# Batch-norm with ReLU on one core: all stores from GpSimd's queue, and the rows loaded in rising order

## The chip, the cores and the metric

The kernel runs on one core of one Trainium2 chip. The metric is the device time of one execution in microseconds (us), as the median of several runs. A profile is taken of one execution. Its span runs from the first instruction of the program to the last.

## The reference

The input x has 32 x 128 x 32 x 32 float32 values (16.78 MB). For each channel c the output is

```
normalized = (x - running_mean[c]) / sqrt(running_var[c] + eps)
out = maximum(normalized * gamma[c] + beta[c], 0)
```

So each value is multiplied by a scale of its channel, a bias of its channel is added, and negative values become 0. Every byte of x is read once, and as many are written.

## The kernel before

x is seen as 4096 rows (batch by channel) of 1024 values (4 KB). They are cut in two halves, t = 0 and t = 1, of 128 partitions with J = 16 rows each, so that partition p of half t holds 16 rows that follow each other in memory (64 KB). Row j of all 128 partitions together is 0.52 MB. All of x has its own place in SBUF (32 times 4 KB a partition), the results overwrite it, and no buffer is used twice.

TILES (L16) lists pieces (t, a, b): rows a to b of half t. The order of the list is the order of the loads and of the work: (0, 0, 2), (0, 2, 4), then all of half 1, then (0, 4, 12) and (0, 12, 16). The loads are issued by SP (L56), one DMA a piece, unless LOAD_CUTS cuts it. They are 1, 1, 8, 4 and 2 MB, and SP issues them all within the first 8 us.

Meanwhile four small DMAs on ScalarE's queue (L63) fetch the channels' parameters, a matmul (L78) spreads them over the partitions, and ScalarE's square root (L86) and four VectorE operations (L88 to L94) make scale_t and bias_t, with one column for each j.

Then ScalarE goes through the pieces in order. For each row it runs one ACTIVATE in place (L102), relu(scale * x + bias), of 128 x 1024 values; a row in HALVES is done as two of 128 x 512. After the last row of a piece, and ahead of each row in STORE_CUTS, it issues a DMA of the finished rows to the output (L110). There are seven stores, of 0.5, 0.5, 1, 4, 4, 4 and 2 MB. The order on ScalarE is the order written (manual_schedule, L96). For the other engines a scheduler sets it.

A DMA's share of one partition is one contiguous run (4 KB times its rows). The 16 DMA engines of the core carry all queues: q1 with SP's loads, q10 with ScalarE's DMAs. At the end SP waits for all DMAs (L144), and then all engines pass a barrier.

Of the kernel before, what the change touches and what calls it, by code (L numbers as in the profile page):

```python
# [1 line left out]

# [4 lines left out]


F32 = mybir.dt.float32
ACTF = mybir.ActivationFunctionType  # L10

J = 16

TILES = ((0, 0, 2), (0, 2, 4), (1, 0, 16), (0, 4, 12), (0, 12, 16))  # L16

LOAD_CUTS = set()
STORE_CUTS = {(0, 1), (1, 8)}

HALVES = {(0, 0)}


@with_exitstack
def kernel(
    ctx: ExitStack,
    tc: tile.TileContext,
    x: bass.AP,
    gamma: bass.AP,
    beta: bass.AP,  # L30
    running_mean: bass.AP,
    running_var: bass.AP,
    eps: bass.AP,
    out: bass.AP,
):
    nc = tc.nc
    B, C, H, W = x.shape
    HW = H * W
    P = nc.NUM_PARTITIONS
    assert C % J == 0 and P % (C // J) == 0 and (B * C) % (P * J) == 0  # L40
    Q = C // J
    T = B * C // (P * J)

    xr = x.rearrange("b c h w -> (b c) (h w)").rearrange("(t p j) w -> t p j w", p=P, j=J)
    outr = out.rearrange("b c h w -> (b c) (h w)").rearrange("(t p j) w -> t p j w", p=P, j=J)

    data = ctx.enter_context(tc.tile_pool(name="data", bufs=1))
    params = ctx.enter_context(tc.tile_pool(name="params", bufs=1))
    psum = ctx.enter_context(tc.tile_pool(name="psum", bufs=1, space=bass.MemoryType.PSUM))

    tiles = []
    for t, a, b in TILES:
        xt = data.tile([P, b - a, HW], F32, name=f"x{t}_{a}")
        cuts = [a] + [j for j in range(a + 1, b) if (t, j) in LOAD_CUTS] + [b]
        for c, d in zip(cuts, cuts[1:]):
            nc.sync.dma_start(out=xt[:, c - a : d - a, :], in_=xr[t, :, c:d, :])  # L56
        tiles.append((t, a, b, xt))

    raw = params.tile([Q, 4, J], F32, name="raw")
    for k, src in enumerate((running_var, gamma, running_mean, beta)):
        nc.scalar.dma_start(out=raw[:, k, :], in_=src.rearrange("(q j) -> q j", j=J))  # L63
    eps_t = params.tile([P, 1], F32, name="eps_t")
    nc.vector.memset(eps_t, float(eps))  # L65
    rep = params.tile([Q, P // Q, Q], F32, name="rep")
    nc.gpsimd.memset(rep, 1.0)  # L67
    nc.gpsimd.affine_select(  # L68
        out=rep,
        in_=rep,  # L70
        compare_op=mybir.AluOpType.is_equal,
        fill=0.0,
        base=0,
        pattern=[[0, P // Q], [-1, Q]],
        channel_multiplier=1,
    )
    cols = psum.tile([P, 4, J], F32, name="cols")
    nc.tensor.matmul(  # L78
        cols.rearrange("p k j -> p (k j)"),
        rep.rearrange("q r s -> q (r s)"),  # L80
        raw.rearrange("q k j -> q (k j)"),
        start=True,
        stop=True,
    )
    std_t = params.tile([P, J], F32, name="std_t")
    nc.scalar.activation(out=std_t, in_=cols[:, 0, :], func=ACTF.Sqrt, bias=eps_t[:, 0:1], scale=1.0)  # L86
    rstd_t = params.tile([P, J], F32, name="rstd_t")
    nc.vector.reciprocal(out=rstd_t, in_=std_t)  # L88
    scale_t = params.tile([P, J], F32, name="scale_t")
    nc.vector.tensor_mul(out=scale_t, in0=cols[:, 1, :], in1=rstd_t)  # L90
    ms_t = params.tile([P, J], F32, name="ms_t")
    nc.vector.tensor_mul(out=ms_t, in0=cols[:, 2, :], in1=scale_t)  # L92
    bias_t = params.tile([P, J], F32, name="bias_t")
    nc.vector.tensor_sub(out=bias_t, in0=cols[:, 3, :], in1=ms_t)  # L94

    with tc.manual_schedule(engines={mybir.EngineType.Activation}):  # L96
        for t, a, b, xt in tiles:
            first = a
            for j in range(a, b):
                step = HW // 2 if (t, j) in HALVES else HW  # L100
                for w in range(0, HW, step):
                    nc.scalar.activation(  # L102
                        out=xt[:, j - a, w : w + step],
                        in_=xt[:, j - a, w : w + step],
                        func=ACTF.Relu,
                        bias=bias_t[:, j : j + 1],
                        scale=scale_t[:, j : j + 1],
                    )
                if j + 1 == b or (t, j + 1) in STORE_CUTS:
                    nc.scalar.dma_start(  # L110
                        out=outr[t, :, first : j + 1, :], in_=xt[:, first - a : j + 1 - a, :]
                    )
                    first = j + 1


# [1 line left out]
_INS = ['x', 'gamma', 'beta', 'running_mean', 'running_var', 'eps']  # L117
_OUTS = [((32, 128, 32, 32), 'float32')]

_NUMBERS = {'eps': 1e-05}  # L120


# [26 lines left out]
```

## Time and profile before

| | |
|---|---|
| median of 7 runs | 83.98 us (83.89 to 84.2) |
| the profiled execution | 83.83 us |
| its span | 82.1 us |
| ScalarE busy | 38.8 us (47%) |
| ScalarE, 33 ACTIVATEs of L102 | 37.3 us |
| VectorE, TensorE, GpSimd busy | under 1 us each |
| read and written | 16.78 MB and 16.78 MB |
| mean rate over the span | 409 GB/s |

How to read it: the profile's engine rows count compute alone. A DMA is seen in three other places: the instruction that issues it (under half a microsecond on its queue), the packets that the 16 DMA engines move later, and the landing, when its semaphore has its full count and a waiting instruction can go on. From issue to landing a 4 MB store here takes 19.6 us, since it waits for its turn.

### The profile page before, as it was taken

The page shows a single profiled execution, that of the slowest core. Times are in us where ns is not written, and L with a number is a line of the kernel's source. Part 1 is how long each engine was busy: PE and PEld are TensorE (multiplying, and loading weights), DVE is VectorE, ACT ScalarE, POOL GpSimd, SP SyncE. Part 2 cuts the span into 40 slices and gives each one's busy share as a digit, 9 for nine tenths or more (in the row PEclk, how much of TensorE's full clock was granted, in tenths as well). Part 3 has the DMA queues.
Part 4 walks back from the last instruction along what each step waited for, and adds up shares of the span by engine and source line. Part 5 has one row for each costly group of instructions (what it writes and reads, how often), then busy time and mean ns, then how long its engine had stood idle before and what let it go on. Part 6 is the DMA issues. An engine that isn't in the chain of part 4 may idle for free.

```text
span 82.1 us, 119 instructions
## 1 busy us (share of the span) xinstructions
PE 0.7 (1%) x2; PEld 0.5 (1%) x2; DVE 0.8 (1%) x5; ACT 38.8 (47%) x35; POOL 0.8 (1%) x6
## 2 busy tenths in 40 slices
PE   0002000000000000000000000000000000000000
PEld 0002000000000000000000000000000000000000
DVE  0000300000000000000000000000000000000000
ACT  0600377600000199997999989997991000000000
POOL 3000000000000000000000000000000000000000
DMA  1999990999929797969989998996996998997992
GB/s 40 367 419 707 511 511 0 511 543 543 447 96 543 319 511 319 575 287 455 407 359 463 519 399 367 511 495 271 511 511 271 495 511 351 415 511 343 423 407 104
DMA packets 1792, 33.56 MB, mean 409 GB/s; under 512 B 256, under 2 KB 256, under 8 KB 512
## 3 DMA queue, kind: packets, MB, share of 16 engines
q1 hardware_dynamic: 720, 16.78, 48.7%
q10 hardware_dynamic: 1072, 16.78, 47.6%
HBM read 16.78 MB, written 16.78 MB: 409 GB/s over the span
## 4 chain that ended last, share of the span: by engine, by line
ACT 37%; DMA 33%; issue 3%; ACTq 1%; SPq 1%
ACT x L102 37%; DMA x<-in_x_dram 33%; ACTq L110 1%; SPq L56 1%
## 5 line engine op out<-in xcount | busy, mean ns | idle before, releaser
L102 ACT ACTIVATE x<-x,bias_t,scale_t 128x1024 f32<-128x1024 f32 (+1 forms) x33 | 37.3, 1205 | 15.9 <-DMA x<-in_x_dram 12.7
L86 ACT ACT_TABLE_LOAD x1 | 1.3, 1283 | 2.6 <-issue 2.6
L86 ACT ACTIVATE std_t<-cols,eps_t 128x16 f32<-128x16 f32 x1 | 0.3, 274 | 4.5 <-PE cols L78 4.5
L78 PE MATMUL cols<-raw,rep 8*128 8x64 f32 x2 | 0.7, 430 | 7.7 <-DMA raw<-in_beta_dram 7.7
L78 PEld LDWEIGHTS cols<-raw,rep 8*128 8x128 f32 x2 | 0.5, 308 | 7.7 <-issue 7.7
L68 POOL TENSOR_SCALAR_AFFINE_SELECT rep<-rep 8x128 f32<-8x128 f32 x1 | 0.4, 394 | 0.1
L88 DVE RECIPROCAL rstd_t<-std_t 128x16 f32<-128x16 f32 x1 | 0.3, 253 | 7.8 <-ACT std_t L86 7.8
L67 POOL MEMSET rep<- 8x128 f32 x1 | 0.2, 196 | 0.3 <-POOLq L130 0.3
L90 DVE TENSOR_TENSOR scale_t<-cols,rstd_t 128x16 f32<-128x16 f32 x1 | 0.2, 175 | 0.1
L92 DVE TENSOR_TENSOR ms_t<-cols,scale_t 128x16 f32<-128x16 f32 x1 | 0.2, 175 | 0.0
L94 DVE TENSOR_TENSOR bias_t<-cols,ms_t 128x16 f32<-128x16 f32 x1 | 0.2, 175 | 0.0
L130 POOL MEMSET const-bfloat16-1.0<- 128x1 bf16 x1 | 0.1, 107 | 0.0
L130 POOL MEMSET const-uint8-127<- 128x1 uint8 x1 | 0.1, 107 | 0.0
L130 POOL MEMSET const-float32-0.0<- 128x1 f32 x1 | 0.1, 104 | 0.3 <-issue 0.3
L130 POOL MEMSET const-float32-1.0<- 128x1 f32 x1 | 0.1, 104 | 0.0
L65 DVE MEMSET eps_t<- 128x1 f32 x1 | 0.1, 59 | 0.9 <-PEq L130 0.9
## 6 DMA issues: line engine op xcount, KB each, us to landing
out_dram<-x ACTq DMA_DIRECT2D x3, 4096.0 KB, 19.6
x<-in_x_dram SPq DMA_DIRECT2D x1, 4096.0 KB
x<-in_x_dram SPq DMA_DIRECT2D x2, 1024.0 KB, 5.6
x<-in_x_dram SPq DMA_DIRECT2D x1, 2048.0 KB
out_dram<-x ACTq DMA_DIRECT2D x1, 2048.0 KB, 19.4
out_dram<-x ACTq DMA_DIRECT2D x2, 512.0 KB, 21.2
out_dram<-x ACTq DMA_DIRECT2D x1, 1024.0 KB, 31.6
raw<-in_running_var_dram ACTq DMA_DIRECT2D x1, 0.5 KB
```

What stands on the lines that cost most here:

```text
L56: nc.sync.dma_start(out=xt[:, c - a : d - a, :], in_=xr[t, :, c:d, :])
L67: nc.gpsimd.memset(rep, 1.0)
L68: nc.gpsimd.affine_select(out=rep, in_=rep, compare_op=mybir.AluOpType.is_equal, fill=0.0, base=0, pattern=[[0, P // Q], [-1, Q]], channel ...
L78: nc.tensor.matmul(cols.rearrange("p k j -> p (k j)"), rep.rearrange("q r s -> q (r s)"), raw.rearrange("q k j -> q (k j)"), start=True, s ...
L86: nc.scalar.activation(out=std_t, in_=cols[:, 0, :], func=ACTF.Sqrt, bias=eps_t[:, 0:1], scale=1.0)
L88: nc.vector.reciprocal(out=rstd_t, in_=std_t)
L90: nc.vector.tensor_mul(out=scale_t, in0=cols[:, 1, :], in1=rstd_t)
L92: nc.vector.tensor_mul(out=ms_t, in0=cols[:, 2, :], in1=scale_t)
L94: nc.vector.tensor_sub(out=bias_t, in0=cols[:, 3, :], in1=ms_t)
L102: nc.scalar.activation(out=xt[:, j - a, w : w + step], in_=xt[:, j - a, w : w + step], func=ACTF.Relu, bias=bias_t[:, j : j + 1], scale=sc ...
L110: nc.scalar.dma_start(out=outr[t, :, first : j + 1, :], in_=xt[:, first - a : j + 1 - a, :])
L130: nc = _bacc.Bacc("TRN2", target_bir_lowering=False, num_devices=1)
```

## The change

All stores are issued by GpSimd (POOL) in place of ScalarE, in an order that is written out, too. The pieces now rise in size: (0, 0, 2), (0, 2, 4), (0, 4, 8), (0, 8, 16), and then all of half 1. Half 1 is loaded by two DMAs of 8 rows (LOAD_CUTS). Loads are 1, 1, 2, 4, 4 and 4 MB. The cut (1, 8) leaves STORE_CUTS, so there are six stores, of 0.5, 0.5, 1, 2, 4 and 8 MB, and the last of them holds all 16 rows of half 1. Row 1 of half 0 is done in two halves, like row 0.

```
-TILES = ((0, 0, 2), (0, 2, 4), (1, 0, 16), (0, 4, 12), (0, 12, 16))
+TILES = ((0, 0, 2), (0, 2, 4), (0, 4, 8), (0, 8, 16), (1, 0, 16))
 
-LOAD_CUTS = set()
-STORE_CUTS = {(0, 1), (1, 8)}
+LOAD_CUTS = {(1, 8)}
+STORE_CUTS = {(0, 1)}
 
-HALVES = {(0, 0)}
+HALVES = {(0, 0), (0, 1)}
...
-    with tc.manual_schedule(engines={mybir.EngineType.Activation}):
+    with tc.manual_schedule(engines={mybir.EngineType.Activation, mybir.EngineType.Pool}):
...
                 if j + 1 == b or (t, j + 1) in STORE_CUTS:
-                    nc.scalar.dma_start(
+                    nc.gpsimd.dma_start(
                         out=outr[t, :, first : j + 1, :], in_=xt[:, first - a : j + 1 - a, :]
                     )
```

## The prediction

> **What bounds the kernel now.** I read the page's slices and queues first, to see whether the DMA engines ever rest.
>
> ```profile
> DMA  1999990999929797969989998996996998997992
> ...
> q1 hardware_dynamic: 720, 16.78, 48.7%
> q10 hardware_dynamic: 1072, 16.78, 47.6%
> HBM read 16.78 MB, written 16.78 MB: 409 GB/s over the span
> ```
>
> q1 carries the loads, which SP issues, and q10 the stores, which ScalarE issues. Together their packets take 96.3% of 82.1 us on all 16 engines: 39.98 us of loads and 39.08 us of stores, 79.06 us in all. (A 0 or 2 in a slice is no hole. A large packet is counted where it starts.) The first load packet starts at about 1.7 us. 1.7 + 79.1 = 80.8, and what is left to 82.1 is the end of the program. So **the DMA engines are full from the first load to the last store**. The kernel is bound by the sum of its transfers. The chain of waits seems to say otherwise:
>
> ```profile
> 1.71 26.71 DMA x<-in_x_dram
> ...
> 57.19 0.13 ACT x L102
> 57.32 1.02 issue
> 58.34 3.49 ACT x L102 x3
> ```
>
> It ends at 61.8 us, with the last store's ScalarE work, because the chain follows engines and not queues. The 20 us behind it are stores that wait for their turn. ScalarE idles 12.7 us before the 8 MB load lands at 28.4 us, which costs nothing as long as the queues are full.
>
> Then I read the queues by stretches, for the price of a packet and for how the two queues share an engine. The columns are packets, MB, and time as a share of 16 engines in the stretch. 10 to 28.4 us, then 28.4 to 38.6, then 38.6 to 46.9, then 56.8 to 82.1:
>
> ```profile
> q1 hardware_dynamic: 128, 6.82, 87.5%
> q10 hardware_dynamic: 96, 0.39, 5.2%
> ```
> ```profile
> q1 hardware_dynamic: 114, 3.67, 83.5%
> q10 hardware_dynamic: 124, 0.44, 10.6%
> ```
> ```profile
> q1 hardware_dynamic: 158, 2.10, 63.1%
> q10 hardware_dynamic: 216, 1.59, 45.3%
> ```
> ```profile
> q10 hardware_dynamic: 416, 9.96, 91.3%
> ```
>
> MB divided by share times stretch gives rates: loads of tile 1 (64 KB of a partition in a packet) 6.82 / 16.1 us = 424 GB/s; loads mostly of rows 4 to 12 (32 KB) 3.67 / 8.52 = 431; loads of rows 12 to 16 (16 KB) 2.10 / 5.24 = 401; stores of 4 KB 0.39 / 0.957 = 407 and 0.44 / 1.08 = 407; large stores alone 9.96 / 23.1 = 431. One engine has a sixteenth, so a 32 KB packet takes 32768 / 26.9 = 1.22 us and a 4 KB one 0.16 us. In the second stretch the queues' times stand 83.5 to 10.6, or 7.9 to 1, and the packets 8 to 1 in size. So **each engine takes one packet of each queue in turn**, and a queue of small packets gets little. That is why the loads are nearly done at 46.9 us while most stores wait.
>
> **The change, part by part.** The bytes are the same: 16.78 MB in, 16.78 MB out.
>
> *Load order and sizes.* Tile 1 now comes last, as two 4 MB loads, and the first half as 1, 1, 2 and 4 MB. The 64 KB load packets go, and 8.39 MB of 32 KB packets stands for them. At 431 instead of 424 GB/s this is 19.79 - 19.46 = 0.33 us less. Mixed with stores, though, the 16 KB loads ran at 401 GB/s, so loads vary by more than this with what runs beside them. I bound the load side by -0.7 us (16 KB loads at full rate as well: 2.10 MB at 431 saves 0.37) and +0.4 us (that loss repeated), and take 0.
>
> *When each row is ready.* Loads alone end at 1.7 + 40.0 = 41.7 us. Store packets are taken from about 11.3 us, when ScalarE finishes row 0. From there some 26 load packets are left (24 of 32 KB, 2 of 16 KB), so at most 26 store packets come between: 16 of 4 KB (0.16 us each), 8 of 8 KB (0.31) and 2 of 16 KB (0.62), 6.3 us in all. The loads end by 48.0 us and have landed by 48.5 (in the trace of before the last load packet ends near 46.0 and its semaphore is full at 46.4). ScalarE, at 9.16 / 8 = 1.145 us a row, has done the other 24 rows: rows 8 to 16 of the first half land near 23 us and are done near 32, the next eight land near 34 and are done near 43. The last eight take until 48.5 + 9.2 = 57.7.
>
> *The last store.* STORE_CUTS loses (1, 8), so all of tile 1 leaves by one 8.39 MB store that waits for the last row, at 57.7 us. Is there work for the engines until then? Loads and the five earlier stores (8.39 MB, half of 39.08) keep them full to 1.7 + 40.0 + 19.5 = 61.2 us. With 0.4 us for the issue (ScalarE's stores take 0.34 to 0.37) and 1 us to the first packet (SP's first load is issued at 0.81 us and moves at 1.7), the store's packets are there at 59.1, so **2 us are to spare and nothing is lost**. The same cover hides the new wait. If it is gone, each us later costs one us. Behind the waiting stores on POOL stand only later stores, since its own work ends at 1.5 us.
>
> *Issue from POOL.* Seven issues of 0.34 to 0.37 us, and five pauses between rows (2.2 us in the list of waits), leave ScalarE. They are worth nothing, since ScalarE isn't on the path; what is late next is the DMA queue, as before. POOL's six issues have no row. I bound one by 0.1 us (POOL's shortest work) and 0.59 us (the longest issue in the trace, a parameter load's). Both stay under the cover above; I take 0.4. SP's six loads still leave early: the fifth and sixth wait for a parameter load and for the first x load, as the last two did before (3.6 and 1.5 us in SP's waits), with over 8 MB queued ahead of them.
>
> *Store packets from POOL's queue.* Before has no transfer from this queue. From below, they are as ScalarE's: 431 GB/s, 0 us (nothing in the trace ran faster). From above, all are as the 4 KB ones: 16.78 / 0.407 = 41.2 us against 39.1, so +2.1 us. The shapes are those of ScalarE's stores (4 KB to 64 KB of a partition), so I take the near row, 0, and keep +2.1 for the range. The Trainium skill, "DMA: Bandwidth & Descriptors", section Latency and other measured facts, says that DMA engines 7 and 15 are usually slower for GpSimd's transfers, with a cause that it calls a guess. In this trace no engine has such transfers, and by this rule the sum would gain an unknown part of a store's time on two engines.
>
> *The end of the program.* SP waits for every DMA semaphore before the last barrier.
>
> ```profile
> L144 SPq EVENT_SEMAPHORE  x7: 17/28/28, 57.1 to 82.1; - x7
> L144 POOLq DRAIN  x3: 34/77/489, 1.0 to 81.9; - x3
> L144 SPq DRAIN  x3: 7/7/7, 81.4 to 81.7; - x3
> ```
>
> Five of the seven are such waits, and the last store is the last of them. In the instruction order of the changed program there are eight, the last store's is the first, and seven follow it: 28 ns each is 0.2 us, and with the gap to the drain that follows the last wait now (about 65 ns from start to start) 0.46 us. I take **+0.35 us**. A longer drain of POOL's queue adds between 0 and 0.4 us (489 for 77 ns); I take 0.
>
> **Sum:** 0 + 0 + 0 + 0.35 = +0.35 us on the profiled 83.83 us (span 82.1, and 1.73 around it, which stay), 84.18. The median of the runs is 0.15 above the profiled one, so 84.33, say **84.3 us, +0.4%**.
>
> **Rivals.**
>
> *Loads get cheaper (faster), 83.6 us.* The load side gives its -0.7 us and the end costs 0.35: -0.35. For it speaks that stores kept their rate and only loads varied (401 to 431). Against it, that loads beside stores are no rarer in the new order.
>
> *Stores run in poorer packets, 86.4 us.* +2.1 + 0.35. For it: nothing shows how POOL's queue cuts a row. Against it: the same contiguous runs gave packets of their full size on two other queues. Half of the loss gives 85.4.
>
> *The stores take more than a packet in a turn (slower), 95.4 us.* This is a stall at one place, ahead of the 8.39 MB store. If the stores get two packets or more for each load packet, all five earlier ones (40 packets an engine, 20 turns) fit among the 26 load packets. The loads then end when all else is done, at 61.2 us. The engines idle for 0.5 (landing) + 9.2 (eight rows) + 1.4 (issue, first byte) = 11.1 us, and the time is 83.98 + 11.1 + 0.35 = 95.4. It decides from loads that end after about 50 us. Against it: the 7.9 to 1 above. For it: that ratio is of ScalarE's queue, and POOL's is another. The Trainium skill, "DMA: Bandwidth & Descriptors", section Queues, rings and completion order, says that an engine empties a whole packet of one ring before it turns, and that a packet has 9 to 17 descriptors typically. By the page a store's share on one engine (8 partitions) would be one turn, and the sum would be this rival's; by the row of before, with one descriptor a turn, it is 84.3.
>
> *Nothing to measure, 84.0 us.* The end's cost and a load gain of 0.3 cancel.
>
> **How the numbers follow.** A difference under 0.2% (0.17 us) can't be told from none here. Chances: forecast 0.38 (84.1 to 84.7; 0.05 of it lies within 0.2%), cheaper loads 0.26, poorer packets 0.16, stall 0.12, nothing 0.08. Slower: 0.33 + 0.16 + 0.12 = 0.61. Same: 0.05 + 0.08 = 0.13. Faster: 0.26. The range from 83.3 (load side at its best) to 86.5 (all packets as 4 KB ones) leaves out the stall and a little below, some 0.17. The likeliest case alone is 84.1 to 84.7.
>
> **What would show it.** Right: DMA busy for 79 us without a hole, loads done before 50 us, the 8.39 MB store issued near 56 to 58 us, seven waits of SP behind the last landing. Wrong: an empty slice before the last store (stall); a store rate under 431 GB/s, or packets smaller than a row group (poorer packets); a load share under 48% of the span (cheaper loads).

## The result and the profile after

The changed kernel takes 84.39 us (median of 14 runs, 84.21 to 84.56) against 83.99 (37 runs of before). The ratio is 1.0044, 95% interval 1.0034 to 1.0054. The forecast was 84.3. The profiled execution took 84.40 us, with a span of 82.7.

The page's slices and queues of the changed kernel:

```profile
ACT  0600499994059998299991299991000000000000
POOL 3000032202000000200000000002000000000000
DMA  1999996979696969797998999899699569999900
...
q1 hardware_dynamic: 864, 16.78, 48.3%
q0 software_dynamic: 864, 16.78, 47.2%
q10 hardware_dynamic: 64, 0.00, 0.0%
```

The stores are on q0 now, and only the parameters are left on q10. Loads take 48.3% of 82.69 us, 39.96 us (before 40.01 in the trace's own sum), and stores 39.0 (before 39.0). Counted packet by packet, at least 16 packets, as many as there are engines, are under way at every moment from 3 us to 78.5 us, shortly before the last packets start, so no gap is seen there. The bound is the same as before.

The last store's cover held, as the rows of POOL and ScalarE show:

```profile
23.71 9.16 ACT L102 ACTIVATE x<-x,bias_t,scale_t 128x1024 f32<-128x1024 f32 x8 [4.28 <-DMA x<-in_x_dram]
33.16 0.53 POOL L110 DMA_DIRECT2D out_dram<-x  x1 [12.90 <-ACT x L102]
34.65 9.16 ACT L102 ACTIVATE x<-x,bias_t,scale_t 128x1024 f32<-128x1024 f32 x8 [1.78 <-DMA x<-in_x_dram]
46.93 9.16 ACT L102 ACTIVATE x<-x,bias_t,scale_t 128x1024 f32<-128x1024 f32 x8 [3.13 <-DMA x<-in_x_dram]
56.38 0.53 POOL L110 DMA_DIRECT2D out_dram<-x  x1 [22.69 <-ACT x L102]
```

Groups of eight rows start at 23.7, 34.7 and 46.9 us, and the last store is issued at 56.4. Its first packet moves at 61.24, when the store ahead of it is through on the first engine.

How the two queues share an engine, in the stretches 28.4 to 38.6 and 56.8 to 82.1 us:

```profile
q1 hardware_dynamic: 141, 4.10, 93.2%
q0 software_dynamic: 133, 0.54, 13.0%
```
```profile
q0 software_dynamic: 209, 9.99, 91.2%
```

93.2 to 13.0 is 7.2 to 1, for 32 KB packets beside 4 KB ones (and a few of 8 KB at the end of the stretch). POOL's queue too gets one packet for one. 9.99 MB in 23.07 us is 433 GB/s, and in the trace all 128 packets of 64 KB took 2418 ns. So POOL's packets are neither poorer nor more in a turn.

The end of the program grew. In the next rows an EVENT_SEMAPHORE of SP is one of its waits, a DRAIN is an instruction at which an engine stops near its end, and RANGE_CLEAR is POOL's clearing of the semaphores. The three figures are the shortest, median and longest in ns, then come the first and last start in us. The instructions of L144:

```profile
L144 SPq EVENT_SEMAPHORE  x10: 17/28/46762, 34.6 to 82.6; - x10
L144 POOLq EVENT_SEMAPHORE  x4: 17/17/17, 82.0 to 82.6; - x4
L144 POOLq DRAIN  x3: 34/102/25311, 56.4 to 82.4; - x3
L144 SPq DRAIN  x3: 7/7/7, 81.9 to 82.2; - x3
L144 POOLq EVENT_SEMAPHORE_RANGE_CLEAR  x1: 139/139/139, 82.3 to 82.3; - x1
```

SP's first wait lasts 46.8 us, up to the last store's landing at 81.38 us. Then come seven more, which start 59 to 68 ns apart, and SP's drain starts at 81.89, 0.51 us after the landing; in before it started at 81.37, 0.08 us after the landing. From the last landing to the end of the span it is 1.31 us in place of 0.83, **0.48 us more**. Another line matters later: POOL's own drain starts at 56.4 us and lasts 25.3 us, until 81.67, 0.29 us after the landing. So it too waits for the store. Two rows of before stand against these:

```profile
L144 ACTq DRAIN  x2: 8/80/153, 62.2 to 81.7; - x2
L144 POOLq EVENT_SEMAPHORE_RANGE_CLEAR  x1: 96/96/96, 81.7 to 81.7; - x1
```

ScalarE's drain in before starts at 62.2 us, with its stores under way until 81, and lasts 0.15 us: it does not wait for them. The clearing of the semaphores took 96 ns there and takes 139 now.

### The profile page after: what moved, and what is told of

It is laid out like the page before. It is cut to its first block, busy times and chain, and to the rows that moved or that the text cites. A ratio compares the mean times of both kernels' runs of the same rounds, so it can differ in the third digit from the quotient of the medians.

```text
span 82.7 us, 125 instructions
## 1 busy us (share of the span) xinstructions
PE 0.7 (1%) x2; PEld 0.5 (1%) x2; DVE 0.8 (1%) x5; ACT 38.7 (47%) x36; POOL 4.2 (5%) x12
## 3 DMA queue, kind: packets, MB, share of 16 engines
q1 hardware_dynamic: 864, 16.78, 48.3%
## 4 chain that ended last, share of the span: by engine, by line
DMA 56%; issue 11%; POOLq 1%
DMA x<-in_x_dram 56%; POOLq L144 1%; POOLq L110 0%
## 5 line engine op out<-in xcount | busy, mean ns | idle before, releaser
L110 POOL DMA_DIRECT2D out_dram<-x x6 | 3.4, 559 | 52.1 <-ACT x L102 52.1
```

The source lines that it names most:

```text
L110: nc.gpsimd.dma_start(out=outr[t, :, first : j + 1, :], in_=xt[:, first - a : j + 1 - a, :])
```

## The experiments

Every run gives the ratio to before with its 95% interval. "The end" is the time from the last landing to the end of the span in the run's own trace (before: 0.83 us).

| run | stores from | us | ratio | the end, us |
|---|---|---|---|---|
| changed kernel | POOL | 84.39 | 1.0044 (1.0034 to 1.0054) | 1.31 |
| e9, the same again | POOL | 84.41 | 1.0050 (1.0037 to 1.0063) | 1.31 |
| e1 changed order | ScalarE | 83.52 | 0.9942 (0.9923 to 0.9961) | 0.83 |
| e8, the same again | ScalarE | 83.74 | 0.9972 (0.9961 to 0.9983) | 0.83 |
| e2 order of before | POOL | 84.46 | 1.0051 (1.0034 to 1.0067) | 1.38 |
| e12, the same again | POOL | 84.43 | 1.0058 (1.0037 to 1.0078) | 1.38 |
| e3 eight waits behind | POOL | 84.50 | 1.0051 (1.0033 to 1.0068) | 1.40 |
| e4 two waits behind | POOL | 84.20 | 1.0025 (1.0014 to 1.0037) | 1.19 |
| e5 last row late | POOL | 90.47 | 1.0771 (1.0755 to 1.0787) | 1.31 |
| e6 last row late | ScalarE | 89.54 | 1.0661 (1.0645 to 1.0677) | 1.05 |
| e7 small loads | POOL | 89.29 | 1.0629 (1.0611 to 1.0646) | 1.31 |
| e10 before, half 1 in two loads | ScalarE | 84.32 | 1.0037 (1.0025 to 1.0049) | 0.93 |
| e11 one first load | ScalarE | 83.93 | 0.9997 (0.9986 to 1.0007) | 0.90 |

The theory was that the waits of SP behind the last store's wait are the cost. The rivals were the order of the loads, and POOL's queue itself, in flight or at the end.

**The two parts alone: e1 and e2, then e8, e9 and e12.** e1 is the changed kernel with

```
-                    nc.gpsimd.dma_start(
+                    nc.scalar.dma_start(
```

and ScalarE alone in the manual schedule, as in before.

> The changed kernel's order, sizes and cuts, with all stores issued from ScalarE's queue again. In the order of the program SP's wait for the last store is then the last of five, so no other DMA wait stands behind it. Theory (the waits of SP at the end cost the 0.4 us): the 0.43 us between the last landing and SP's drain go, and with the 0.06 us of POOL's longer clearing of semaphores the time is 84.39 - 0.49 = 83.9, ratio to before 0.999 (0.997 to 1.001). Rival 1 (the order and sizes of the loads cost it): 84.4, ratio 1.0044. Rival 2 (stores from POOL's queue move worse): 84.0 too, so this run doesn't tell it from the theory.

It measured 83.52 us, under the theory's range: not equal to before, but faster. e2 is the kernel before with the opposite edit at L110 and POOL in the manual schedule:

> The kernel before with one thing changed: its seven stores are issued from POOL's queue, the order and the sizes stay. SP has nine waits at the end, the last store's is the first, so eight stand behind it. Theory: 8 x 0.06 = 0.48 us and 0.06 us of clearing on 83.99, that is 84.5, ratio 1.006 (1.005 to 1.008). Rival 1 (load order): 84.0, ratio 1.000. Rival 2 (POOL's packets): 84.4, with more than 39.1 us of store time on the 16 engines.

It measured 84.46, near the theory's 84.5. Since e1 is 0.87 us under the changed kernel where the end explains 0.48, I ran e1 and the changed kernel again on one chip, and e2 again later:

> The kernel of the first run again (the changed kernel's order, stores from ScalarE's queue), beside the changed kernel itself in the next run, to size the two parts of the change on one chip. First time: 83.52 against 84.0 before, 0.87 under the changed kernel, of which the end of the program explains 0.48. If the theory of the end is the whole price of POOL's queue, the two runs differ by 0.5 us (0.4 to 0.6) and this one gives 83.8 to 83.9; if POOL's queue costs something in flight as well, by 0.8 to 0.9, and this one gives 83.5.

> The changed kernel as it is, on the same chip as the run before: 84.4, ratio 1.0044 (1.0034 to 1.0054).

> The kernel before with its stores from POOL's queue, again, to see whether the queue costs anything beside the end of the program. The end is 0.55 us longer than before's in this kernel's first trace (1.38 against 0.83 from the last landing). If that is all, 84.5, ratio 1.0065 (1.005 to 1.008); if a cost in flight of 0.2 us stands beside it, as in the changed order, 84.7, ratio 1.009; the first time gave 1.0051, under both.

They gave 83.74, 84.41 and 84.43. The order alone is worth -0.48 us the first time and -0.19 the second, -0.3 over the 12 runs together (median 83.70). The queue alone costs +0.46 and +0.51 in the order of before, which the longer end (0.55) covers in full. In the changed order it costs 0.87 and 0.67, which is 0.2 to 0.4 more than the end's 0.48. The spans of e8 and e9 differ by 0.83 us, 0.35 more than the end; 0.15 of this is load time (39.90 and 40.05 us) and 0.11 a later start of the engines, in the mean. Load times of equal kernels differ by as much from run to run (39.96 and 40.10 in e2 and e12), so what causes this rest is open.

SP's waits at the end in e8:

```profile
L144 SPq EVENT_SEMAPHORE  x7: 17/28/12417, 34.9 to 81.9; - x7
L144 POOLq DRAIN  x3: 34/78/487, 1.0 to 81.7; - x3
L144 SPq DRAIN  x3: 7/7/7, 81.2 to 81.5; - x3
```

There are seven in place of ten. SP's first drain starts 0.08 us after the landing, and no drain of POOL is long, since POOL has issued nothing that it must wait for.

**The number of waits behind the last one: e3 and e4.** Tiny loads on POOL's queue move the last store to another semaphore, and so to another place in SP's list:

```
+    spare = params.tile([Q, 2, J], F32, name="spare")
+    for k in range(2):
+        nc.gpsimd.dma_start(out=spare[:, k, :], in_=beta.rearrange("(q j) -> q j", j=J))
```

> The changed kernel with two tiny loads (0.5 KB each, into a spare tile) issued from POOL's queue at the start, which take the first two semaphores of that queue. The last store moves to another semaphore; its wait is still SP's first of now nine, eight stand behind it. Theory: one wait more than in the changed kernel, 0.06 us, so 84.45, ratio 1.0051 (1.004 to 1.0065). Rivals 1 and 2: 84.4. Read against the next run.

e4 has 3 in place of 2.

> The same with three tiny loads in place of two: the last store now takes the queue's first semaphore again, which SP waits for as the seventh of nine, so only two waits stand behind it. Nothing else moves. Theory: six waits fewer than with two tiny loads, 6 x 0.06 = 0.37 us, so 84.1, ratio 1.001 (1.000 to 1.0025). Rivals 1 and 2, and a cost of POOL's queue at the end of the program: 84.4 to 84.5, the same as with two tiny loads.

They measured 84.50 and 84.20: six waits fewer are worth 0.30 us by the medians. The theory held where its rivals said no difference. (The two profiled executions stand the other way round, 84.22 us for e3 and 84.38 for e4: e3's is the fastest of its six, with 0.13 us less load time.) But by the traces the end is shorter by only 0.21 us, and not by 0.37. The rows of SP and POOL in e4, where before's L144 is L147:

```profile
L147 SPq EVENT_SEMAPHORE  x11: 17/28/18928, 62.2 to 82.6; - x11
L147 POOLq EVENT_SEMAPHORE  x4: 17/17/17, 81.9 to 82.6; - x4
L147 POOLq DRAIN  x3: 40/102/25422, 56.5 to 82.4; - x3
L147 SPq DRAIN  x3: 7/7/7, 81.7 to 82.2; - x3
```

The last store landed at 81.48 us and SP's drain started 0.18 us later, but POOL's drain went on to 0.41 us after the landing, and POOL's first instruction of the barrier comes only behind it, at 81.9 us. So a second cost lies beneath the waits: POOL's drain ends 0.29 us after the landing in the changed kernel, where SP's waits (0.51 us) hide it, and it is what ends last when the waits are few. Of the 0.48 us, e4 gets back 0.12. The other 0.36 belongs to a queue of POOL's with work in it: its drain, and the longer clearing of semaphores (139 ns for 96). In e4 the drain ends 0.12 us later than in the changed kernel, for a reason that the traces don't show. With the changed kernel's own drain about 0.24 in place of 0.36 would be left, an estimate (0.29 us, and the 0.77 from the drain's end to the end of the span in e4, against 0.83) that no run tests.

**The cover of the last store: e5 and e6.** In both, ahead of the last row:

```
+                if (t, j) == (1, 15):
+                    for _ in range(8):
+                        nc.scalar.activation(
+                            out=spare,
+                            in_=xt[:, 0, :],
...
```

> The changed kernel with eight more ACTIVATEs of 128x1024 on ScalarE ahead of the last row (one row of half 1 into a spare tile, which nobody reads): the output is the same, and the last store is issued 8 x 1.145 = 9.2 us later, at 65.6 us in place of 56.4. Theory (the DMA engines have other work until 61.2 us, which covers the last store's wait): the first 4 us cost nothing, from the issue to the first packet POOL needs 1 us, and the engines are idle for about 65.6 + 1 - 61.2 = 5.4 us; 89.8, ratio 1.069. Rival (ScalarE's time is not covered): +9.2 us, 93.6, ratio 1.114. Third (other work covers all of it): 84.4.

> The same eight ACTIVATEs, and the stores issued from ScalarE's queue. The first packet after the issue stands in the open here, as with POOL's queue in the run beside it, so the difference of the two is the price of an issue from POOL on the path. Theory: issue 0.34 us and 0.5 us to the first packet against 0.53 and 0.5 or more for POOL, and no waits at the end: 0.5 us of the end and 0.2 to 0.7 us of the issue less than with POOL's queue, 88.6 to 89.1. Rival (an issue costs the same from both queues): 89.3, less by the end alone.

They measured 90.47 and 89.54: e5 0.7 us over its theory, and e6 over both of its values. Both forecasts took a spare row at 1.145 us, and it took 1.27. The slices of e5, with its last row and issue:

```profile
DMA  3899999969799699998899999895009999994690
```
```profile
64.77 1.22 ACT L112 ACTIVATE x<-x,bias_t,scale_t 128x1024 f32<-128x1024 f32 x1
66.29 0.53 POOL L120 DMA_DIRECT2D out_dram<-x  x1 [32.69 <-ACT x L112]
```

Now there is a true hole, two slices of 0 at 62 to 66 us. The issue moved by 66.29 - 56.38 = 9.9 us, and not by 9.2, and the time by 6.1. So 3.8 us were covered. That is also what the changed kernel's trace says: its last store's packets could have come 1.10 us after the issue, at 57.5, and came at 61.24. In e6 the last issue is

```profile
64.93 1.23 ACT L112 ACTIVATE x<-x,bias_t,scale_t 128x1024 f32<-128x1024 f32 x1
66.19 0.34 ACTq L120 DMA_DIRECT2D out_dram<-x  x1
```

and the first packet moves at 67.03; in e5 it moves at 67.39. From the end of the row that is 0.87 us with ScalarE's queue and 1.40 with POOL's, 0.53 apart; from the start of the issue 0.84 and 1.10. In e5 that first packet is 0.36 us later than in e6, and the end is 0.26 us longer (1.31 and 1.05): 0.62 of the 0.64 us between the two spans (88.61 and 87.97). The medians differ by 0.93, in the theory's 0.7 to 1.2 and over the rival's 0.5; 0.3 of it the two traces don't show. Nor do they show why e6's end is longer than e8's (1.05 for 0.83): ScalarE's last drain starts 0.31 us later there. The Trainium skill, "DMA: Bandwidth & Descriptors", section Latency and other measured facts, gives about 0.6 us to the first byte for ScalarE's and SP's kind of queue and about 1 us for GpSimd's. The order of the two agrees with the 0.84 and 1.10 us here. In the changed kernel this costs nothing, as its last store stands in a queue that isn't empty.

**The turns: e7.**

```
-LOAD_CUTS = {(1, 8)}
+LOAD_CUTS = {(1, 2), (1, 4), (1, 6), (1, 8), (1, 10), (1, 12), (1, 14)}
```

> The changed kernel with the loads of half 1 cut into eight DMAs of two rows (8 KB of a partition in place of 32 KB), all else the same. Theory (an engine takes one packet of each queue in turn, whatever its size): there are 64 turns of half 1's loads in place of 16, all five earlier stores get through beside them, the loads end at about 60 us in place of 46.6, and the last store waits for the last rows with nothing else to move: idle 3 to 4 us and 0.4 us of poorer packets, 88 (87 to 89.5), ratio 1.05. Rival (the engines share by bytes): the loads end where they did, 84.4 to 84.9.

It measured 89.29 us. The slices, and the queues between 40 and 62 us:

```profile
DMA  3899999899599999999897989999209999998290
```
```profile
q1 hardware_dynamic: 699, 5.11, 55.0%
q0 software_dynamic: 160, 4.19, 44.2%
```

The loads ended at 62.2 us in place of 46.6, with the same bytes, since their 8 KB packets got one turn for one 16 or 32 KB packet of a store. Then the engines stood idle for 4.5 us. The loads took 40.73 us for 39.96. This is the mechanism of the prediction's stall rival, brought about by the sizes of the loads. The time was 1.3 us over my 88 and within its range, as the last rows landed later than I had it (62.2 us for 60). The Trainium skill, "DMA: Bandwidth & Descriptors", section Queues, rings and completion order, calls 9 to 17 descriptors in a packet typical; here each turn moved one run of one partition, on SP's, ScalarE's and POOL's queues.

**Where the order's gain is from: e10 and e11.** e10 is the kernel before with `LOAD_CUTS = {(1, 8)}`.

> The kernel before with one thing changed: half 1 is loaded by two DMAs of 8 rows (32 KB packets in place of 64 KB). It looks for where the order's gain is from. Two waits of SP stand behind the last store's here, 0.12 us. If the 64 KB load packets cost the 0.3 to 0.4 us (2468 ns in the mean where the quickest took 2418), 83.99 - 0.35 + 0.12 = 83.75, ratio 0.997; if the gain is from the 16 KB loads beside stores or from the larger last store, 84.1, ratio 1.0014.

It measured 84.32, over both. The 64 KB load packets aren't the cause. The 32 KB ones in their place are slower by the byte: 1250 ns in the mean (419 GB/s over 16 engines) for 2468 ns (425 GB/s) of the 64 KB ones in before, whose own 32 KB loads took 1216. Loads took 40.27 us in all, 0.26 more than before. e11 is e1 with `TILES = ((0, 0, 4), (0, 4, 8), (0, 8, 16), (1, 0, 16))` and `STORE_CUTS = {(0, 1), (0, 2)}`.

> The first run's kernel with the first two loads in one DMA of four rows (16 KB packets), the stores unchanged: a candidate for the best. It saves 8 KB packets, 16 x 0.309 - 8 x 0.611 = 0.06 us, and whatever the 8 KB packets at the start took over 309 ns (0.24 to 0.56 us in the traces so far), and pays one wait of SP at the end, 0.06 us. Half of that excess gone: 83.3; all of it due to the start itself: 83.5.

It measured 83.93, worse than e1 and e8 and over both values that I had. The 16 KB packets in the first 4 us took 0.57 us over their quickest in sum on an engine, the 8 KB ones of the other kernels 0.24 to 0.56. So in this one trace the slow start comes with the start, whatever the size. Loads took 40.06 us in all, for 39.84 and 39.90 in e1 and e8.

## Why the prediction was right, and where it was only lucky

**The time, the side and the bound** were right. The engines are full in both kernels and 79 us of packets set the time. The traces show no compute, issue or wait that leaves the engines empty between the first loads and the last store.

**"When each row is ready" and "the last store"** were right. The loads ended at 46.6 us (bound 48.0), the last group of rows started at 46.9, the issue was at 56.4 (bound 57.7), and 3.8 us were to spare where the bounds gave 2. e5 shows the price of the cover, and e7 that it goes with the loads' turns.

**"Store packets from POOL's queue", 0,** was right: 39.0 us in both, 433 GB/s. That some engines would be slower with POOL's stores isn't seen: in the changed kernel all 64 KB packets took the same 2418 ns.

**"Issue from POOL", 0,** was right on the path; one issue is 0.53 us where I took 0.4, and the first, at 0.69, is over my bound of 0.59.

**"The end of the program", +0.35,** has the right mechanism and a size too small: +0.48 in the trace. The seven waits gave 0.42 (59 to 68 ns each, my upper bound was 0.46), and the clearing of semaphores and its barrier 0.06, which I left out. And I took a longer drain of POOL's at no price, which came true only because the waits lie on top of it: e4 shows 0.36 of cost with the waits nearly gone.

**"Load order and sizes", 0,** was mis-sized: -0.3 us by e1 and e8 (-0.19 to -0.48). The rival "cheaper loads" had its place; the range of -0.7 to +0.4 held it. Of the gain, the traces of e1 and e8 show 0.1 to 0.2 in load time and 0.07 in store time. My lower bound had two parts. The 16 KB loads did come to their full rate: 611 ns a packet in the changed kernel for 652 in before, 0.33 us where I had 0.37. The 64 KB packets' 0.33 did not come: I took the 431 GB/s of before's 32 KB loads for all of them, and in the changed kernel they ran at 422 (1243 ns), under the 425 of the 64 KB ones; e10 shows the same. Nor is it stores beside them that slow the 16 KB loads: in e10 they stood beside stores, too, and took 612 ns.

So it was luck that the sum came so near, for three misses cancel in part: the order's -0.3 that I put at 0, an end of 0.48 that I put at 0.35, and 0.2 to 0.4 us of POOL's queue in this order which the runs show twice and I can't place. The forecast's sum is nearer than its terms.

e1, the changed order with ScalarE's stores, beats both kernels: 0.9942 and 0.9972 of before in two sets of runs.

## What to carry to other kernels

When the queues are never empty, ask of each edit only whether it changes the bytes' packet time, empties the queues, or lengthens what comes behind the last landing; moving the issue to POOL changed the last, by 0.5 us, and in one of the two orders 0.2 to 0.4 us more whose cause is open. Look at the order of the waits at the end of the program: a DMA that lands last should be waited for last, and POOL's drain is short where POOL issues no DMAs (at most 0.49 us in e8). The sizes of packets decide who gets the engines while two queues are full, so small early stores let large loads through, and small loads let the stores go first (in e7 the loads ended at 62.2 us in place of 46.6).

## What the runs showed of the hardware that I had not expected

A wait of SP that is already fulfilled costs 59 to 68 ns, so eight semaphores in a poor order cost half a microsecond. A drain of POOL with its stores under way ends 0.29 to 0.41 us after the last landing, while ScalarE's, with its own stores under way, was through in 0.15 us. Load packets vary (32 KB ones from 1213 to 1553 ns in the changed kernel, 1243 in the mean), while every store packet of a size takes the same time there to 1 ns, from 159 ns for 4 KB to 2418 for 64 KB (up to 2465 in e5 to e7, where the last store starts on empty engines); what slows single loads stays open, and by it two kernels of equal bytes can be 0.2 to 0.3 us apart.
